# Gated linear attention issued by two generators, with level 2 of its scan issued beside level 4, a new order and overlap for the windowed attention, and separate tiles for one stage's norm factors

## The chip, the cores and the metric

One core of a Trainium2 chip runs the whole kernel. The metric is device time in microseconds (us) of one execution; lower is better. The kernel before takes 2370.8 us (median of three runs, 2370.01 to 2372.45).

## The reference

Two token sequences of width 1024, one of 2048 and one of 512 tokens, pass through two layers with the same weights, all in float32.

- Layer 0: one input projection feeds two attention branches. Branch A is gated linear attention: 4 heads of 128 channels, scanned forward and backward, each key weighted by a data-dependent decay: `scores[i,j] = sum_d q[i,d] k[j,d] exp(b[i,d] - b[j,d])`, where `b` is the running sum of the log decay; beyond a chunk the sum is carried by a state `S = exp(b_last) * S + k^T v`. Branch B is softmax attention over a window of 128 tokens to either side: 8 query heads share 2 key/value heads, with a relative-position bias and a sink logit. Each branch is multiplied by its own SiLU gate, and both go through one output projection.
- Layer 1: `y = W_out( silu(z) * B * conv3(C * h) )` with a depthwise convolution of width 3 along the tokens.
- After each layer: `x = LayerNorm(alpha * x + sublayer(x)) * g + b`, with the layer's own g and b.

## The kernel before, in words

**Work and tiles.** The 2560 tokens are five groups of 512 (group 4 is the short sequence) and 20 chunks of 128. Every dense projection is done in fp32r as three products: a matrix is cast to a high part (`wh`, or `hi` of the activations), the rest is a low part (`wl`, `lo`), and high*high, low*high and high*low are summed in PSUM. A step of 128x512 is one TensorE matmul; nearly all of the matmuls are of this form.

**The dense order.** `run` (L2103) has a fixed list of stages: for each group from 4 to 0 a token projection (`tok`), then a channel projection (`ch`, 21 units of 24 matmuls); between these the output projection of group 4 (`oe4`); then layer 1 of group 4 (`one`), and `oe0`, `oo4`, `oe1`, `oe2`, `pair0`, `oe3`, `oo0`, `pair1`, `oo1`, `oo2`, `oo3`. `oe` and `oo` are output projections of layers 0 and 1; `pair` does layer 1's input projection for two groups by a Strassen-like scheme of 7 products.

**What fills in.** Everything else runs as Python generators beside the dense order. `Flow` keeps a model clock for each engine (`Model.note` adds fixed costs for each instruction). After every few dense matmuls `Flow.pump` (L337) lets each generator issue its next piece if the model says that its inputs are there and VectorE and ScalarE are not over 4 to 5 us ahead. So the program order on each engine is settled when the program is built; at run time each engine takes its instructions strictly in that order, TensorE too, and a matmul whose input is late holds up all that follow it. `new` and `take` hand out tiles of small rings by the model's idle times: `md` (8 tiles of 128x512, called `mids`), `y` (4 of 128x1024, called `large`), `P` (4), `ps` and `acc` (4 PSUM banks each).

**Gated linear attention.** `gla_stream` (L1454) takes the chunks backwards, 19 to 16 and 15 to 0, one after the other. `inside` (L1186) does a chunk: it forms `Q` (q times decay, both directions), then goes through the scan levels s = 1, 2, 4, 8, 16, 32, 64. At each level it issues a burst of narrow matmuls (`blocks`: 16 fp32 products of 32 rows by 32 columns, two instructions each), grows `K` and `Q` by the decay totals on VectorE, and selects the level's block into `acmp`. Level 8 is already put off: `qm`, a copy of `Q`, is taken by ScalarE and its 32 instructions are issued in the burst of level 16 (L1238, L1308). After level 64 the same generator goes on with the chunk's tail: it completes `A`, transposes `K` (`turn`, L1327), multiplies with `v`, and updates the state `S`. Only then does the next chunk's `Q` start. When a sequence is done, `along` (L1402) runs forward over it and writes `mix_s`.

**Windowed attention.** `swa_front` (L1510) takes a block of 128 queries, one key/value head at a time: scores on TensorE, bias and maximum on VectorE, exponentials on ScalarE. `best` (L1518) chooses the next block: highest group first, until the mark `done_e1_0` (the last projection of group 0 is stored), then lowest block first. `swa_back` (L1579) transposes each of the up to three 128-wide parts of P, splits it into `ph` and `pl`, and issues the value products of part n after the transposes of part n+1.

**Norms.** `norms` (L1700) normalizes a stage's four rows of tiles with `ln_g` and `ln_b`, two tiles for the layer in hand. `ln_load` (L729) reloads them after `x1_0` (to layer 1), after `y_4` (to layer 0) and after `x1_3` (to layer 1).

Of the kernel before, what the change touches and what calls it, by code (L numbers as in the profile page):

```python
# [10 lines left out]
F32 = mybir.dt.float32  # L11
# [251 lines left out]
class Flow:  # L263
# [32 lines left out]
    def flush(self, everything=False, name=None):  # L296
        now, keep = [], []
        for one in self.late:
            (now if everything or name in one[2] or (name is None and one[0] <= self.t) else keep).append(one)
        self.late = self.model.late = keep  # L300
        for one in now:
            one[1]()
# [74 lines left out]
class Trunk:  # L377
    def __init__(self, tc, nc, I, y_out, ctx):
# [35 lines left out]
        self.blocks = []  # L414
# [3 lines left out]
        self.normed, self.turn = None, 0  # L418
# [150 lines left out]
    def dense_ch(self, xh, xl, w=None, last=True):  # L569
# [3 lines left out]
        p = self.pd()  # L573
# [13 lines left out]
        if last:  # L587
            self.drop(wl)
        return p
# [86 lines left out]
    def setup(self):  # L676
# [9 lines left out]
        self.dtot = c.tile([128, NC, 4], F32, name="dtot")  # L686
# [29 lines left out]
    def setup_late(self):  # L716
# [10 lines left out]
        yield from self.ln_load(0)  # L727

    def ln_load(self, layer):  # L729
        for t, n in zip(self.ln, ("ln_g", "ln_b")):  # L730
            yield from self.calm()
            self.nc.sync.dma_start(t[:], self.I[n][layer:layer + 1].broadcast_to([128, D]))
# [446 lines left out]

    def gla_load_k(self, c):  # L1180
        K = self.e((128, 2, 512), "KK")
# [4 lines left out]
    def inside(self, c, first, last, ld, K, ahead):  # L1186
# [3 lines left out]
        Q = self.e((128, 2, 512), "QQ")  # L1190
# [10 lines left out]

        acmp = self.sm((128, 4, 32), "acmp")
# [17 lines left out]
        def grow_k(s):  # L1220
# [12 lines left out]
        Sb = self.bst if not last else None  # L1233
        wait = []
        for li, s in enumerate((1, 2, 4, 8, 16, 32, 64)):
            n = 512 // s
            pls = []
            if s in (8,):  # L1238
# [3 lines left out]
            else:  # L1242
# [14 lines left out]
                for lt, t, qm in wait:  # L1257
# [3 lines left out]
                    self.drop(qm)  # L1261
# [24 lines left out]
                kms.pop(s, None)  # L1286
# [14 lines left out]
            if s not in (8,):  # L1301
                grow_q()
# [5 lines left out]
            if s in (8,):  # L1308
                grow_q()
# [13 lines left out]
        nc.vector.tensor_copy(self.dtot[:, c], mk(end, 4, [[1, 4]]))  # L1323
        ahead(0)
        self.flow.defer(lambda: nc.sync.dma_start(self.qf_s[c], Q[:, 1]), Q)

        def turn(i):  # L1327
# [3 lines left out]
            t = self.e((128, 4, 128), "km", bufs=2)  # L1331
# [3 lines left out]
        def grow(t):  # L1335
            pv = self.pw((128, 4, 128))
            for h in range(4):
                nc.tensor.matmul(pv[:, h], t[:, h], v[:, h * 128:h * 128 + 128], start=True, stop=True)
            return pv

        kf = kb = None
        if not last:
            yield from self.bank()
# [5 lines left out]
                                  acmp[:].unsqueeze(2).broadcast_to(wide))  # L1349
        if not first:  # L1350
            yield from self.bank()
            kb = turn(1)
        ahead(1)
# [10 lines left out]
        if not first:  # L1364
# [6 lines left out]
            else:  # L1371
                for h in range(4):
                    nc.vector.scalar_tensor_tensor(Sn[:, h], Sb[:, h], mk(end, h, [[1, 1]]), pv[:, h],
# [8 lines left out]
        yield [Q]  # L1382
# [19 lines left out]
    def along(self, c, first, last, ld, ahead):  # L1402
# [13 lines left out]
        if not last:  # L1416
# [4 lines left out]
            else:  # L1421
                for h in range(4):
                    nc.vector.scalar_tensor_tensor(Sn[:, h], Sf[:, h], self.dtot[:, c, h:h + 1], m[:, h],
# [29 lines left out]

    def gla_stream(self):  # L1454
        for g in (4, 3, 2, 1, 0):
# [3 lines left out]
            cs = list(range(4 * g + 3, 4 * g - 1, -1))  # L1459
            ld, K = self.gla_load(cs[0]), self.gla_load_k(cs[0])  # L1460
            nxt = {}
            for i, c in enumerate(cs):
                yield [*ld, K]

                def ahead(n):
                    if i < 3:
                        nxt[n] = (self.gla_load, self.gla_load_k)[n](cs[i + 1])
                yield from self.inside(c, *ends(c), ld, K, ahead)
                ld, K = nxt.get(0), nxt.get(1)
            if 4 * g > c0:  # L1470
                continue
            self.bst = None
            ld = K = None
            nxt.clear()
# [35 lines left out]
    def swa_front(self):  # L1510
# [7 lines left out]
        def best():  # L1518
# [4 lines left out]
            key = (lambda c: c) if "done_e1_0" in done else (lambda c: (-(c // 4), c))  # L1523
# [3 lines left out]
        while left:  # L1527
# [10 lines left out]
            for kv in range(2):  # L1538
# [3 lines left out]
                Pt = self.e((128, 4, 385), "P", bufs=4)  # L1542
# [36 lines left out]
    def swa_back(self):  # L1579
# [17 lines left out]
        for n in range(40):  # L1597
# [19 lines left out]
            old = None  # L1617
            for kb in range(nk):
# [586 lines left out]
```

## Time and profile before

| | |
|---|---|
| runs, median of 3 | 2370.8 us |
| the profiled execution's own time | 2370.12 us |
| its span, first to last instruction | 2368.1 us |
| TensorE matmul busy | 2343.9 us, 99% |
| TensorE weight loads busy | 1951.8 us, 82% |
| VectorE / ScalarE / GpSimd busy | 1582.8 / 1226.1 / 1418.4 us |

PE is TensorE, DVE VectorE, ACT ScalarE, POOL GpSimd, SPq the queue of SyncE, which issues the DMAs. Matmuls are pipelined, and the duration shown for one includes its time in the pipeline: what one costs is read from start to start, and "busy" does not mean that the engine advances at full rate.

### The profile page before, as it was taken

What the parts mean: (1) busy time and instruction counts of PE and PEld (TensorE: products, weight loads), DVE (VectorE), ACT (ScalarE), POOL (GpSimd) and SP (SyncE); (2) the same over time, 40 slices, a digit from 0 to 9 for tenths busy, and PEclk for the clock granted to TensorE, in tenths of its full rate; (3) what the DMA queues carried; (4) which work ended last, traced back from release to release, by engine and by line L of the source; (5) the groups of instructions that cost most, each with busy time, mean ns of one, the idle gap of its engine ahead of it and who ended that gap; (6) DMA issues with size and microseconds to landing.
All of it is one profiled execution on the core that took longest, in us unless ns stands there. A gap on an engine that the chain in (4) does not pass through costs nothing.

```text
span 2368.1 us, 43087 instructions
## 1 busy us (share of the span) xinstructions
PE 2343.9 (99%) x15830; PEld 1951.8 (82%) x15830; DVE 1582.8 (67%) x2699; ACT 1226.1 (52%) x2363; POOL 1418.4 (60%) x1610
## 2 busy tenths in 40 slices
PE   8999999999999999999999999999999999999998
PEld 8888889888988888888888888878888877888887
DVE  2267756767767677577776467876566587656567
ACT  4666776656576645665577532543334343333431
POOL 5454435443444444444444467898887689988674
PEclk9999999999999999999999999999999999999999
DMA  7977686676667657675478777232124633221573
GB/s 230 295 226 233 221 269 229 209 221 221 218 194 236 223 173 242 197 218 161 158 245 268 266 261 243 92 116 89 52 78 140 217 105 103 73 72 58 175 242 121
DMA packets 275057, 437.37 MB, mean 185 GB/s; under 512 B 21360, under 2 KB 160240, under 8 KB 274848
## 3 DMA queue, kind: packets, MB, share of 16 engines
q1 hardware_dynamic: 274848, 434.64, 56.5%
q8 instruction: 125, 2.05, 0.4%
q14 instruction: 84, 0.69, 0.1%
HBM read 319.72 MB, written 114.84 MB: 184 GB/s over the span
## 4 chain that ended last, share of the span: by engine, by line
PE 87%; DVE 5%; POOL 4%; DMA 2%; issue 1%; ACT 1%; SPq 0%; POOLq 0%; DVEq 0%; ACTq 0%
PE acc L242 71%; PE ps L242 17%; POOL wl L242 1%; POOL wh L242 1%; DVE st L242 1%; DVE bst L242 1%; DVE y L242 1%; POOL md L242 0%; SPq L242 0%; DVE QQ L242 0%; DVE P L242 0%; DVE KK L242 0%; DMA K<-kb_s 0%; DMA mix_s<-gb 0%; DMA op_s<-QQ 0%
## 5 line engine op out<-in xcount | busy, mean ns | idle before, releaser
L242 POOL TENSOR_TENSOR wl<-ws,wh 128x256 fp32r<-128x256 f32 (+1 forms) x912 | 750.7, 855 | 711.4 <-PE acc L242 478.0
L242 PE MATMUL acc<-st,wh 128*128 128x512 f32 x3160 | 828.5, 395 | 2.8 <-DVE pr L242 2.0
L242 PEld LDWEIGHTS acc<-st,wh 128*128 128x128 f32 x3160 | 580.9, 188 | 121.0 <-issue 3.1
L242 PE MATMUL acc<-st,wl 128*128 128x512 f32 x1744 | 471.9, 395 | 2.8 <-POOL wl L242 1.9
L242 PE MATMUL acc<-wh,st 128*128 128x512 f32 (+1 forms) x1680 | 389.4, 371 | 7.9 <-ACT st L242 6.4
L242 PEld LDWEIGHTS acc<-st,wl 128*128 128x128 f32 x1744 | 320.8, 188 | 68.0 <-POOL wl L242 4.1
L242 PEld LDWEIGHTS acc<-wh,st 128*128 128x128 f32 x1680 | 300.2, 189 | 55.1 <-ACT st L242 6.4
L242 ACT CAST wh<-ws 128x1024 fp32r<-128x1024 f32 (+2 forms) x252 | 249.0, 989 | 184.2 <-DMA ws<-in_w_oo 55.9
L242 PE MATMUL acc<-wl,st 128*128 128x512 f32 (+1 forms) x840 | 209.0, 368 | 0.6 <-POOL wl L242 0.5
L242 ACT ACTIVATE md<-md 128x512 f32<-128x512 f32 x264 | 164.7, 631 | 20.5 <-DVE md L242 14.9
L242 PEld LDWEIGHTS acc<-wl,st 128*128 128x128 f32 x840 | 150.7, 188 | 23.8 <-POOL wl L242 1.3
L242 DVE SCALAR_TENSOR_TENSOR md<-acc,md 128x512 f32<-128x512 f32 (+1 forms) x113 | 77.0, 683 | 81.5 <-ACT md L242 76.5
L242 DVE TENSOR_TENSOR st<-pr,st 128x512 fp32r<-128x512 f32 x115 | 98.5, 874 | 41.6 <-ACT st L242 41.2
L242 ACT ACTIVATE md<-acc 128x512 f32<-128x512 f32 (+1 forms) x133 | 76.2, 597 | 67.0 <-PE acc L242 66.5
L242 POOL TENSOR_TENSOR wh<-md,wh 128x256 fp32r<-128x256 f32 x118 | 96.7, 842 | 13.6 <-ACT wh L242 13.1
L242 ACT CAST pth<-ps 128x512 fp32r<-128x512 f32 x112 | 65.3, 583 | 73.1 <-PE ps L242 72.3
L242 DVE CUSTOM_DVE_ANT_0 P<-ps,P 128x384 f32<-128x384 f32 (+1 forms) x160 | 79.3, 525 | 29.6 <-PE ps L242 29.0
L242 ACT ACTIVATE P<-P,nm 128x385 f32<-128x385 f32 (+1 forms) x160 | 93.2, 587 | 3.9 <-DVE nm L242 3.9
L242 ACT ACTIVATE mv<-mv,eps 128x1 f32<-128x1 f32 x40 | 11.8, 295 | 151.8 <-DVE mv L242 147.7
L242 PE MATMUL acc<-P,wh 128*128 128x512 f32 x312 | 89.5, 400 | 0.4 <-POOL wh L242 0.4
L242 ACT COPY km<-KK 128x512 f32<-128x512 f32 x80 | 50.8, 635 | 72.2 <-DVE KK L242 50.9
L242 ACT CAST st<-pr 128x512 fp32r<-128x512 f32 x115 | 68.3, 617 | 30.3 <-DMA pr<-mix_s 12.9
(490 smaller groups left out, 4090.2 us busy)
## 6 DMA issues: line engine op xcount, KB each, us to landing
ws<-in_w_ch SPq DMA_DIRECT2D x105, 512.0 KB, 4.4
ws<-in_w_od SPq DMA_DIRECT2D x58, 512.0 KB, 4.2
ws<-in_w_oe SPq DMA_DIRECT2D x40, 512.0 KB, 3.8
ws<-in_w_oo SPq DMA_DIRECT2D x36, 512.0 KB, 3.5
K<-kb_s SPq DMA_DIRECT2D x32, 384.0 KB, 6.3
d_s<-md SPq DMA_DIRECT2D x40, 256.0 KB, 4.2
qb_s<-md SPq DMA_DIRECT2D x80, 128.0 KB, 3.9
tA<-d_s SPq DMA_DIRECT2D x20, 512.0 KB, 5.7
```

What stands on the lines that cost most here:

```text
L242: r = f(*a, **k)
```

## The change

- `inside` now ends after level 64 and puts what the tail needs on a list; a second generator, `gla_behind`, does the tails (`behind`). So the head of the next chunk may run beside the tail of this one. At most two chunks are open between head and the completed `A`.
- Level 2 is treated as level 8 was: `qm` is copied by ScalarE, and level 2's 32 instructions are issued in the burst of level 4.
- `Q` and `K` of a chunk may live in a `y` tile when their own tile is in use; copies of `K` and its transposes come from `md` tiles; loads of q, decay and `K` are issued from levels 4 and 32, the load of `v` by the tail.
- `swa_front` changes to lowest block first at `swa_in0` (the windowed attention's inputs of group 0 are stored), earlier than before. `swa_back` may have two transposed parts under way, and issues a part's value products after its own split.
- Layer 1's norm factors for the stage `y_4` get two `P` tiles of their own (`ln1`), filled after `x1_0`; the reload after `y_4` goes away.
- Some tiles are held explicitly, and `flush` no longer runs an entry twice.

```diff
@@ gla_home, gla_load_k
+    def gla_home(self, tag):
+        done = self.flow.done
+        rows = "swa_in1" in done and "res_x1_4_3" not in done
+        return [(self.e2, tag, 1)] if rows or self.model.spare(tag, 1) else self.large[:1]
-        K = self.e((128, 2, 512), "KK")
+        K = self.take(self.gla_home("KK"), (128, 2, 512))
@@ inside
-        Q = self.e((128, 2, 512), "QQ")
+        while self.free_at(self.gla_home("QQ")) > self.flow.t:
+            yield 0.3
+        Q = self.take(self.gla_home("QQ"), (128, 2, 512))
...
+        while self.open > 1:
+            yield 0.3
+        self.open += 1
...
-                    km = kms[2 * s] = self.e((128, 512), "km", bufs=2)
+                    km = kms[2 * s] = self.take([(self.e2, "km", 2)] + self.mids, (128, 512))
...
-            if s in (8,):
+            if s in (2, 8,):
+                while self.free_at(self.mids) > self.flow.t:
+                    yield 0.3
                 qm = self.m2(hold=True)
...
-            if s not in (8,):
+            if s not in (2, 8,):
                 grow_q()
...
-            if s in (8,):
+            if s in (2, 8,):
                 grow_q()
...
-            if s == 4:
-                v = self.e((128, 512), "v")
-                nc.sync.dma_start(v[:], self.v_s[c])
+            if s in (4, 32):
+                ahead(s)
             yield [Q] if s < 16 else [Q, K]
-        end = tots[128]
+        nc.vector.tensor_copy(self.dtot[:, c], mk(tots[128], 0, [[1, 8]]))
+        self.heads.append((c, first, last, K, Q, base, acmp))
+        self.flow.mark("head_%d" % c)
+    def behind(self, c, first, last, K, Q, base, acmp, v, ahead):
...
-            t = self.e((128, 4, 128), "km", bufs=2)
+            t = self.m2((128, 4, 128), hold=True)
@@ gla_behind
+    def gla_behind(self):
+        nxt = []
+        for c in [*range(19, 15, -1), *range(15, -1, -1)]:
+            yield "head_%d" % c
+            v = nxt.pop() if nxt else self.load_v(c)
+            def ahead():
+                if c not in (0, 16) and "gla_in%d" % ((c - 1) // 4) in self.flow.done:
+                    nxt.append(self.load_v(c - 1))
+            yield from self.behind(*self.heads.pop(0), v, ahead)
@@ swa_front
-            key = (lambda c: c) if "done_e1_0" in done else (lambda c: (-(c // 4), c))
+            key = (lambda c: c) if "swa_in0" in done else (lambda c: (-(c // 4), c))
@@ swa_back
+            def room():
+                return begun < nk and self.model.spare("ps", 4) > 1 and self.free_at([(self.pside, "ps", 4)]) <= self.flow.t
             for kb in range(nk):
+                if not turned:
+                    yield from self.bank()
+                    turn()
+                    begun += 1
+                if room():
+                    turn()
+                    begun += 1
+                pt, ph = turned.pop(0)
+                yield [ph]
...
+                yield [pl, V]
+                value(kb, ph, pl)
@@ norm, norms
-        g, b = self.ln
+        g, b = self.ln1 if one and one[:4] == "y_4_" else self.ln
...
-        if key in ("x1_0", "y_4", "x1_3"):
-            yield from self.ln_load(0 if key == "y_4" else 1)
+        if key == "x1_0":
+            yield "swa_all"
+            for n in range(2):
+                while self.free_at([(self.e2, "P", 4)]) > self.flow.t:
+                    yield 0.4
+                self.ln1.append(self.take([(self.e2, "P", 4)], (128, D)))
+            yield from self.ln_load(1, self.ln1)
+        if key == "y_4":
+            self.drop(*self.ln1)
+        if key == "x1_3":
+            yield from self.ln_load(1, self.ln)
@@ run
         flow.add(self.gla_stream(), rank=1)
+        flow.add(self.gla_behind(), rank=1)
```

## Rows read from the trace of the kernel before

**Rows 1.** The page, busy time, share of the span and instructions of each engine.

```profile
PE 2343.9 (99%) x15830; PEld 1951.8 (82%) x15830; DVE 1582.8 (67%) x2699; ACT 1226.1 (52%) x2363; POOL 1418.4 (60%) x1610
```

**Rows 2.** The page, the chain that ended last, by engine.

```profile
PE 87%; DVE 5%; POOL 4%; DMA 2%; issue 1%; ACT 1%; SPq 0%; POOLq 0%; DVEq 0%; ACTq 0%
```

**Rows 3.** Busy time by stretch: stretch, its length, each engine, PE clock, DMA.

```profile
118.00:355.00 237.00, 237.00 (x2134) 200.75 (x2133) 160.83 (x355) 163.51 (x354) 108.87 (x139) 1.00 0.75 238
355.00:1180.00 825.00, 823.14 (x7857) 691.13 (x7856) 596.59 (x1245) 499.45 (x969) 367.85 (x458) 1.00 0.66 208
```

**Rows 4.** The same view, a stretch of dense work alone.

```profile
1652.00:1711.00 59.00, 59.00 (x260) 48.33 (x259) 33.51 (x42) 23.24 (x33) 48.02 (x51) 1.00 0.18 62
```

**Rows 5.** PE in order of time (start, us, instructions): levels 2 and 4 of a chunk.

```profile
125.78 1.29 PE L242 MATMUL acc<-st,wh 128*128 128x512 f32 x5
127.01 0.46 PE L242 MATMUL ps<-QQ,km 128*32 128x32 f32 x32
127.40 2.11 PE L242 MATMUL acc<-st,wh 128*128 128x512 f32 x8
129.34 1.98 PE L242 MATMUL acc<-st,wl 128*128 128x512 f32 x8
131.25 0.46 PE L242 MATMUL ps<-QQ,km 128*32 128x32 f32 x32
```

**Rows 6.** The same view: levels 8 and 16 of that chunk, in one burst.

```profile
146.50 0.46 PE L242 MATMUL ps<-md,km 128*32 128x32 f32 x32
146.78 0.49 PE L242 MATMUL ps<-QQ,km 128*32 128x32 f32 x32
147.19 0.74 PE L242 MATMUL ps<-K,Q 128*128 128x256 f32 x4
```

**Rows 7.** Groups of PE instructions: count, busy and mean, idle before.

```profile
L242 PE MATMUL ps<-QQ,km 128*32 128x32 f32 x1920 | 28.1, 199 | 1.1 <-ACT pth L242 0.7 <-DVE acmp L242 0.2 <-DVE QQ L242 0.2
```

**Rows 8.** PE in order of time: 128-column products of a tail, then value products.

```profile
301.55 1.06 PE L242 MATMUL ps<-v,km 128*128 128x128 f32 x8
302.36 0.48 PE L242 MATMUL ps<-pth,V 128*128 128x512 f32 x1
302.68 0.40 PE L242 MATMUL ps<-ptl,V 128*128 128x512 f32 x1
```

**Rows 9.** What PE waited for from 118 to 1357 us: total, times, longest.

```profile
PE ps L242 <- ACT pth L242: 0.7, 1, 0.7
...
PE ps L242 <- DVE QQ L242: 0.2, 1, 0.2
```

**Rows 10.** Groups of ACT instructions: the copy of Q that puts level 8 off.

```profile
L242 ACT COPY md<-QQ 128x512 f32<-128x512 f32 x20 | 12.4, 619 | 0.0
```

**Rows 11.** Groups of DVE instructions, one operand in PSUM, then none.

```profile
L242 DVE TENSOR_TENSOR ptl<-ps,pth 128x512 fp32r<-128x512 f32 x112 | 76.3, 681 | 10.8 <-ACT pth L242 10.5
L242 DVE TENSOR_TENSOR QQ<-QQ,tC 128x512 f32<-128x512 f32 x60 | 51.5, 859 | 39.7 <-PE ps L242 39.4
```

**Rows 12.** Busy time by stretch: the most crowded 12 us of VectorE.

```profile
1092.00:1104.00 12.00, 11.69 (x172) 9.00 (x172) 11.69 (x25) 4.73 (x8) 5.82 (x6) 1.00 0.25 71
```

**Rows 13.** SP's queue in order of time, the second reload for x1_1's norms.

```profile
1448.95 0.43 SPq L242 DMA_DIRECT2D ln_b<-in_ln_b  x1
```

**Rows 14.** DVE in order of time, the first use of a reloaded factor.

```profile
1457.87 1.28 DVE L242 SCALAR_TENSOR_TENSOR Q<-Q,mv,ln_g 128x1024 f32<-128x1024 f32 x1
```

**Rows 15.** PE in order of time, the start of pair 0.

```profile
1546.48 1.98 PE L242 MATMUL acc<-st,wl 128*128 128x512 f32 x8
1549.60 0.73 PE L242 MATMUL acc<-st,wl 128*128 128x512 f32 x2 [1.14 <-POOL wl L242]
1551.27 1.08 PE L242 MATMUL acc<-st,wl 128*128 128x512 f32 x2 [0.94 <-DVE acc L242]
1552.15 4.20 PE L242 MATMUL acc<-P,wh 128*128 128x512 f32 x12
...
1556.18 0.39 PE L242 MATMUL acc<-st,wh 128*128 128x512 f32 x1
```

More of the change, by code (lines that the diff above doesn't have):

```diff
@@ L296, in flush @@
     def flush(self, everything=False, name=None):
[L297 to L300, printed above, removed]
+        now = [one for one in self.late if everything or name in one[2] or (name is None and one[0] <= self.t)]
         for one in now:
-            one[1]()
+            if any(one is x for x in self.late):
+                self.late[:] = [x for x in self.late if x is not one]
+                one[1]()
     def force(self, *tiles):
@@ L726, in setup_late, with ln_load @@
         self.ln = [c.tile([128, D], F32, name=n) for n in ("ln_g", "ln_b")]
-        yield from self.ln_load(0)
-    def ln_load(self, layer):
-        for t, n in zip(self.ln, ("ln_g", "ln_b")):
+        yield from self.ln_load(0, self.ln)
+    def ln_load(self, layer, tiles):
+        for t, n in zip(tiles, ("ln_g", "ln_b")):
             yield from self.calm()
@@ L1338, in grow, with place @@
                 nc.tensor.matmul(pv[:, h], t[:, h], v[:, h * 128:h * 128 + 128], start=True, stop=True)
+            self.drop(t)
             return pv
+        def place():
+            yield from self.bank()
+            while self.free_at(self.mids) > self.flow.t:
+                yield 0.3
         kf = kb = None
         if not last:
-            yield from self.bank()
+            yield from place()
             kf = turn(0)
@@ L1349, in inside @@
                                   acmp[:].unsqueeze(2).broadcast_to(wide))
+        self.open -= 1
         if not first:
-            yield from self.bank()
+            yield from place()
             kb = turn(1)
-        ahead(1)
+        self.drop(K)
         yield [A, v] + ([Sb] if Sb is not None else [])
@@ L1381, in inside @@
             self.flow.defer(lambda: nc.sync.dma_start(self.m_s[c], A[:].rearrange("p h t -> p (h t)")), A)
-        yield [Q]
+        self.drop(Q)
+        ahead()
+        self.flow.mark("tail_%d" % c)
     def along_load(self, c, first, last):
@@ L1616, in value, with turn @@
                 nc.tensor.matmul(po[:], vv, pl[:], start=False, stop=(kb == nk - 1))
[L1617 to L1619 removed]
+            turned, begun = [], 0
+            def turn():
                 pt = self.pw((128, 4, 128), hold=True)
                 for gq in range(4):
[L1622 to L1633 removed]
@@ new lines, in swa_back @@
+            for kb in range(nk):
+                if not turned:
+                    yield from self.bank()
+                    turn()
[5 more added lines that the diff above has]
+                yield [ph]
+                pl = self.new(self.e2, (128, 512), F32R, "ptl", 2, True)
+                nc.vector.tensor_tensor(pl[:], pt[:].rearrange("p h t -> p (h t)"), ph[:].bitcast(F32), op=ALU.subtract)
+                self.drop(pt)
+                pt = None
+                if not turned and kb < nk - 1:
+                    yield []
+                    if room():
+                        turn()
+                        begun += 1
+                if kb == nk - 1:
+                    self.drop(Pt)
+                    Pt = None
+                    self.blocks.pop(0)
+                yield [pl, V]
+                value(kb, ph, pl)
+                self.drop(ph, pl)
+                ph = pl = None
```

81 lines of the change are left out of this document (42 added, 39 removed).

## The prediction

> **What bounds the kernel now.** I read the page's busy times first. TensorE's matmuls are busy for 2343.9 of 2368.1 us [rows 1], and the chain that ended last is TensorE for 87% [rows 2]. A better schedule can therefore win little by filling idle time, since only 24 us are idle. But busy is not the same as advancing at full rate, so I next read starts instead of durations. In a stretch of dense work alone 260 matmuls of 512 columns start in 59.00 us [rows 4], which is 0.227 us each. The table by stretch shows the two stretches of linear attention, 118 to 355 and 355 to 1180 us, with TensorE busy for 237.00 of 237 and 823.14 of 825 us, while VectorE is at 68% and 72% and ScalarE at 69% and 61% [rows 3]. So in these 1062 us TensorE's instructions are the bound, and what counts is how many there are and what each costs in its place; work on the other engines is free until it makes TensorE wait. It waits little: from 118 to 1357 us the trace has four waits, 0.7 us the longest and 0.2 the shortest, 1.6 in all [rows 9].
>
> The orders in time show what is slow without being a wait. Around a burst of 32 narrow matmuls [rows 5] five dense matmuls start at 125.78 and the burst at 127.01: 1.23 us for work of 1.135, so 0.095 for entering. The burst runs to 127.40, 0.39. The eight dense matmuls behind it take 1.94 instead of 1.815, 0.125 more, and the next burst comes after 1.91 for eight, again 0.095 for entering. A lone burst costs 0.095 + 0.39 + 0.125 = 0.61 us. Levels 8 and 16, which share a burst of 64, run from 146.50 to 147.19 [rows 6]: 0.69, and with the same entry and the same delay behind it (which these rows don't show for it) 0.91.
>
> **The change part by part.** The sum is made against the profiled execution, 2370.12 us: its span of 2368.1 and 2.0 around it. It is 0.7 below the median of the runs, 2370.8, and I add that at the end.
>
> *Level 2 beside level 4.* Level 2 has a burst of its own now; it will sit in level 4's. The instructions stay: the form has 1920 of them, three groups of 32 for each of 20 chunks (levels 2, 4 and 16) [rows 7]. Two lone bursts, 2 x 0.61 = 1.22, become one of 0.91: 0.31 us for each chunk, 20 x 0.31 = 6.2 us. All of it lies in stretches where TensorE is the bound, so all of it moves the end. It could be less if a joint burst delays the dense work behind it by more: the most that rows allow is that only one entry is saved, 20 x 0.095 = 1.9. I take 6.2, since levels 8 and 16 are the same construction.
>
> The rule that speaks against so much: the Trainium skill, TensorEngine Tiling (Array Packing), Key Properties, says that changing the tiling mode drains the TensorE, and TensorE: Matmul & The Clock Gate, Step-by-step, puts a drain at about 128 cycles. As an estimate from those pages two changes of mode fewer in each chunk are 2 x 0.053 x 20 = 2.1 us (at the 2.4 GHz level), and the sum by that would be 2369.6 with the crowding below. The rows show 0.095 + 0.125 around a lone burst, about twice two such drains, and 0.09 more within (two runs of 0.39 against one of 0.69), so I go by the rows.
>
> The edit adds 20 copies on ScalarE, 0.619 us each by the copy that level 8 already needs, 12.4 us [rows 10]. ScalarE's 39% of free time in the long stretch hides them; without that cover they would be at most 12.4.
>
> *Two generators.* No arithmetic is added. Heads follow each other sooner, tails run beside them, and linear attention gets done earlier. That alone earns nothing: the dense order is unchanged, and TensorE is full whether a burst comes now or later. What it can change is waits. VectorE's work comes closer together. In the most crowded 12 us, with VectorE busy for 11.69, TensorE was busy for 11.69 too, 0.31 lost [rows 12]; over the long stretch it lost 825 - 823.14 = 1.86, 0.03 in 12 us [rows 3]. The new waits stand on TensorE ahead of dense matmuls, everything behind them waits too. From below, the 1.6 us of waits [rows 9] could go. From above, each chunk could pay the longest, 20 x 0.7 = 14. I take three more such crowded stretches, +0.9, near the lower end, because a generator still issues only when the model clock finds its inputs ready.
>
> *Tiles and loads.* `Q` and `K` may take `y` tiles and the turned `K` takes `md` tiles; the loads of q, decay and `K` come earlier on SP's queue, the load of `v` later, in the same number. A load that waits for its tile holds up the weight loads queued behind it on SP, and then GpSimd's low parts and TensorE. The nearest row for a dense stage that lacks a weight's low part is 1.14 us, at the pair's start [rows 15]; once in each of the four token projections from group 3 to 0 that would be 4.6, so 0 to 4.6. I take 0: `Q`'s and `K`'s places are asked for before they are taken.
>
> *Windowed attention.* The number of transposes and value products stays. A tail's eight products of 128 columns and the value product behind them take 302.68 - 301.55 = 1.13 us [rows 8]; less 0.227 that is 0.11 for each, with no visible price for changing between these forms. So their order is worth 0 within TensorE; the ends are the same waits as above. Lowest block first from an earlier mark brings group 0's results sooner, but TensorE has no wait over 0.7 between 118 and 1357, and `oe0` begins before that; nothing there to win.
>
> *Own norm factors.* Two DMAs go, 512 KB each by the tile's size. The second was issued at 1448.95 [rows 13] and a reloaded factor first used at 1457.87, in a VectorE sequence without a gap [rows 14]. So the reload is hidden by the norms before it and `oe1`'s last evictions, and its going is worth 0; without that cover it would be at most the 8.92 us between the two rows. *Held accumulators and flush* add no instruction: 0, and TensorE waits for no bank in the four rows; one such wait would be the 0.94 for DVE's `acc` [rows 15].
>
> Sum: 2370.1 - 6.2 + 0.9 = 2364.8; with 0.7 to the median **2365.5 us**.
>
> **The rivals.**
>
> *A. The gain is eaten or smaller.* Either only entries are saved, 2370.8 - 1.9 + 0.9 = 2369.8 (the place of the skill's drain rule named above), or each chunk pays a new wait of 0.2, the shortest seen [rows 9], 2370.8 - 6.2 + 4.0 = 2368.6. For it: every chunk has new neighbours in the queues, and VectorE's operations on two SBUF tiles take 859 ns where one with an operand in PSUM takes 681 [rows 11], while the model's fixed price is the same for both. Against it: even at 97% VectorE the loss was 0.31 in 12 us.
>
> *B. VectorE becomes the bound where head and tail overlap; slower.* The place is TensorE's narrow bursts of levels 4 to 64, which need VectorE's newest `Q`, `K` and `acmp`. If the model places them too early, each chunk pays about the longest wait, 0.7: 20 x 0.7 = 14, 2370.8 - 6.2 + 14 = 2378.6. It decides from 0.31 a chunk on against the gain, and from (6.2 + 4.7)/20 = 0.55 on for a measurable loss. For it: the 859 against 681 ns, and waits that name `acmp` and `QQ`. Against it: VectorE at 72% leaves 228 us over the long stretch, and its total work does not grow.
>
> *C. The pair's start loses its stall.* From 1546.48 to 1556.18 there are 24 matmuls, worth 5.45 us, in 9.70 [rows 15]: 4.2 lost, to GpSimd's `wl`, VectorE's `acc`, and then to matmuls at 0.33 us each. If the changed order before it removes that: 2361.3. For it: the work in front of the pair loses a reload and changes tiles. Against it: neither waited-for item belongs to the reload or to attention.
>
> *D. The change doesn't do what it says:* if tiles are never free in time, heads and tails stay in sequence; then the +0.9 goes and the rest stands, 2364.6, within the forecast.
>
> **How the numbers follow.** Forecast (with D) 0.54, its own range 2362 to 2368.5; A 0.18; B 0.15; C 0.13. A measurement of this kernel can tell about 0.2%, 4.7 us, from no change, so faster means below 2366.1. Two thirds of the forecast lie there, 0.37, and with C 0.50; the rest of it, 0.17, and A are 0.35; slower is B, 0.15. For the range I take C's end with another 2 us of the waits that could go, 2359, and above it A and the lighter half of B, 2373.
>
> **What would show it.** Level 2 right: narrow matmuls of the form from an `md` copy double from 640 to 1280, those from `QQ` with `km` fall by 640, and 20 of the 32-bursts are gone, with about 6 us less between the starts of the dense stages on either side. Crowding: the waits of TensorE between 118 and 1357, now 1.6, and VectorE's share there; over 11 us more of waits means B. The reload: `x1_1`'s norms no earlier against the end of `oe1`. C: the 24 matmuls at the pair's start. I am wrong if the narrow bursts merge and the stretch up to 1357 doesn't get shorter, or if the end moves by more than 6 us for anything behind it.

## The result, and the profile after

The changed kernel takes 2374.88 us (median of 20 runs, 2371.47 to 2384.03), the kernel before 2369.94 beside it: ratio 1.0025, 95% interval 1.0019 to 1.0032. I had forecast 2365.5, so the change went the other way: 5 us slower in place of 5 us faster. Its profiled execution is one of the longest, 2380.03 us with a span of 2377.9 and a mean granted clock of 0.996, where the four executions at 0.999 took 2371.47 to 2373.13.

The page's busy row for the kernel after, against [rows 1]:

```profile
PE 2343.1 (99%) x15830; PEld 1958.0 (82%) x15830; DVE 1579.3 (66%) x2699; ACT 1235.1 (52%) x2384; POOL 1426.6 (60%) x1610
```

TensorE has the same 15830 matmuls and the same busy time in a longer span. The same stretches as in [rows 3], kernel after, show where it idles: 2.61 us of the first, 8.48 of the second, where before it was 0 and 1.86, with VectorE and ScalarE about as busy as before.

```profile
118.00:355.00 237.00, 234.39 (x2120) 199.66 (x2119) 158.09 (x348) 163.17 (x351) 107.96 (x139) 0.99 0.74 235
355.00:1180.00 825.00, 816.52 (x7831) 690.78 (x7830) 587.84 (x1236) 506.22 (x981) 369.68 (x453) 0.99 0.66 209
```

The join itself did what it should. TensorE in order of time in the same chunk as [rows 5], kernel after; levels 2 (`md`) and 4 (`QQ`) now share a burst:

```profile
132.25 2.43 PE L242 MATMUL acc<-st,wh 128*128 128x512 f32 x10
134.60 0.46 PE L242 MATMUL ps<-md,km 128*32 128x32 f32 x32
134.88 0.49 PE L242 MATMUL ps<-QQ,km 128*32 128x32 f32 x32
135.30 1.65 PE L242 MATMUL acc<-st,wh 128*128 128x512 f32 x6
136.79 1.98 PE L242 MATMUL acc<-st,wl 128*128 128x512 f32 x8
```

Ten dense matmuls take 2.35 us to the burst (2.27 at 0.227 each), the burst 0.70, the six behind it 1.49 (1.362): 0.08 + 0.70 + 0.13 = 0.91, the joint price that I had put together from [rows 5, 6]. The groups of PE instructions, kernel after, show that it happened in all chunks: 1280 narrow matmuls read an `md` copy of Q, 640 before.

```profile
L242 PE MATMUL ps<-md 128*32 128x32 f32 x640 | 9.4, 201 | 0.0
L242 PE MATMUL ps<-md,km 128*32 128x32 f32 x640 | 9.2, 199 | 0.0
```

The bursts merged, and TensorE's idle time in the two stretches grew by 9.2 us, more than the join gives: the sign by which I had said that I would be wrong.

What took it back are waits of PE. The four longest groups of eight, 118 to 1360 us, kernel after (total, times, longest); the eight are 11.8 us, before there were four of 1.6 in all [rows 9]:

```profile
PE acc L242 <- DVE md L242: 4.0, 1, 4.0
PE ps L242 <- DMA K<-kb_s: 2.7, 2, 1.8
PE ps L242 <- DVE y L242: 2.1, 1, 2.1
PE ps L242 <- DVE ptl L242: 1.1, 2, 0.9
```

To add up gains and losses I took from each trace the interval from every matmul's start to the next, less the usual one of its shape (0.227 us for 128x512 [rows 4], 0.153 for 128x336, 0.007 for a narrow one). *Narrow* is what this leaves around and in the narrow bursts (32 and 64 columns wide); *late* is the sum of all intervals more than 0.18 us too long, most of them waits, some of them matmuls at a lower clock. A *place* is a group of late starts close together.

| profiled execution | narrow | late, 118 to 1360 | late, elsewhere | small rest | last matmul starts |
|---|---|---|---|---|---|
| before | 56.3 | 3.0 | 13.7 | 22.5 | 2359.9 |
| after | 51.2 | 16.8 | 14.5 | 23.0 | 2369.7 |
| difference | -5.1 | +13.8 | +0.8 | +0.5 | +9.8 |

(The first matmul starts 0.3 earlier.) This is the profiled execution, 10 us over the one before. The medians are only 4.9 apart, so with the same 5.1 gained an estimate of the loss at the median is about 10. Three places make 12.0 of the 16.8. In each, one matmul at the head of TensorE's queue waits for its input, and everything behind it waits too.

*172 us, 2.3.* PE in order of time, kernel after (start, us, instructions, [idle before <- releaser]):

```profile
172.32 0.46 PE L242 MATMUL ps<-md,km 128*32 128x32 f32 x32
174.84 0.46 PE L242 MATMUL ps<-y,km 128*32 128x32 f32 x32 [2.07 <-DVE y L242]
175.23 0.58 PE L242 MATMUL acc<-wl,st 128*128 128x336 f32 x2
```

VectorE there, kernel after:

```profile
171.07 0.16 DVE L242 SCALAR_TENSOR_TENSOR nm<-mx,nsink 128x4 f32<-128x4 f32 x1
171.16 1.39 DVE L242 SCALAR_TENSOR_TENSOR md<-acc,norm_g,md 128x512 f32<-128x512 f32 x2
172.48 0.55 DVE L242 TENSOR_TENSOR tC<-tB 128x256 f32<-128x256 f32 x1
173.50 0.69 DVE L242 TENSOR_TENSOR y<-y,tC 128x512 f32<-128x512 f32 x1 [0.47 <-DVE tC L242]
174.10 0.68 DVE L242 TENSOR_TENSOR y<-y,tB 128x512 f32<-128x512 f32 x1
```

A joint burst: its level 2 half is issued, its level 4 half needs `Q` (here in a `y` tile) grown by `tB`. That stands on VectorE behind two operations of the dense stage's SiLU and behind the growth of `K` by `tC`, which the edit puts ahead of `Q`'s at level 2. The two growths themselves take 0.69 and 0.68 us. Busy time by stretch behind the wait, kernel after (stretch, length, PE, weight loads, DVE, ACT, POOL, PE clock, DMA):

```profile
174.80:176.00 1.20, 1.16 (x36) 1.07 (x37) 1.17 (x4) 0.86 (x2) 0.00 (x0) 1.00 0.98 297
176.00:178.00 2.00, 2.00 (x10) 1.95 (x9) 2.00 (x6) 1.14 (x4) 0.00 (x0) 0.57 0.23 80
178.00:180.00 2.00, 2.00 (x10) 2.00 (x9) 1.86 (x5) 1.30 (x3) 1.92 (x3) 0.58 0.40 118
```

The wait costs more than itself: after 1.2 us at full clock the granted clock is 0.57 and 0.58 for 4 us.

*378 us, 5.2.* PE in order of time, kernel after:

```profile
377.93 0.86 PE L242 MATMUL acc<-wh,st 128*128 128x336 f32 x4
382.76 1.49 PE L242 MATMUL acc<-wh,st 128*128 128x336 f32 x4 [3.96 <-DVE md L242]
```

VectorE there, kernel after:

```profile
378.19 0.85 DVE L242 TENSOR_TENSOR KK<-KK,tC 128x512 f32<-128x512 f32 x1
378.97 1.03 DVE L242 TENSOR_TENSOR QQ<-QQ,tB 128x512 f32<-128x512 f32 x1
379.92 0.68 DVE L242 SCALAR_TENSOR_TENSOR md<-acc,md 128x512 f32<-128x512 f32 x1
380.52 0.14 DVE L242 SCALAR_TENSOR_TENSOR nm<-mx,nsink 128x4 f32<-128x4 f32 x1
380.59 0.68 DVE L242 SCALAR_TENSOR_TENSOR md<-acc,md 128x512 f32<-128x512 f32 x1
381.96 1.41 DVE L242 SCALAR_TENSOR_TENSOR md<-acc,norm_g,md 128x512 f32<-128x512 f32 x2 [0.69 <-ACT md L242]
```

The token projection needs an accumulator that the SiLU chain of the channel projection still holds; the chain waits on VectorE behind the first head of a group, which grows `KK` and `QQ`. Here too the clock falls. The same view:

```profile
378.00:382.70 4.70, 0.80 (x6) 0.51 (x4) 3.90 (x8) 3.53 (x7) 1.44 (x2) 0.83 0.18 59
382.70:387.00 4.30, 4.24 (x75) 3.82 (x75) 2.52 (x5) 3.18 (x10) 0.00 (x0) 0.50 0.75 163
387.00:391.00 4.00, 4.00 (x23) 3.80 (x24) 3.82 (x8) 2.42 (x4) 2.39 (x4) 0.89 0.93 297
```

The granted clock falls during the wait and is 0.50, the 1.2 GHz level, for the 4.3 us after it, where the four 128x336 products at 382.76 need 1.29 us in place of 0.61.

*1035 us, 4.5.* PE in order of time, kernel after:

```profile
1034.80 1.07 PE L242 MATMUL acc<-st,wl 128*128 128x512 f32 x4
1037.71 0.36 PE L242 MATMUL ps<-K,Q 128*128 128x256 f32 x1 [1.84 <-DMA K<-kb_s]
1038.90 0.86 PE L242 MATMUL ps<-K,Q 128*128 128x256 f32 x5 [0.83 <-DMA K<-kb_s]
```

SP's queue before it, kernel after:

```profile
1032.59 1.22 SPq L242 DMA_DIRECT2D K<-kb_s  x2
1033.92 0.54 SPq L242 DMA_DIRECT2D ws<-in_w_ch  x1
1034.50 0.43 SPq L242 DMA_DIRECT2D gb_s<-md  x1
1034.97 1.60 SPq L242 DMA_DIRECT2D y<-k_s  x2
```

The two loads of the windowed attention's keys were issued at 1032.59 and 1033.20, and the matmuls that need them start at 1037.7 and 1038.9: 5.1 and 5.7 us, beside a head's `K` (`y<-k_s`) and a weight. That is no slow load: the 40 loads `K<-kb_s` of this trace land 3.9/6.6/7.2 us (min/median/max) after their issue, and in the kernel before 5.1/6.4/8.6. The model clock takes at least 3.6 for a load (a constant in `Model.note`), less than any of them. The waits are 2.67 of the 4.5; behind them the clock falls again:

```profile
1040.00:1045.00 5.00, 5.00 (x30) 3.94 (x30) 3.94 (x13) 2.99 (x6) 1.71 (x1) 0.67 0.91 335
```

The three waits are 8.7 us. The lower clock behind them costs about 5.9, an estimate from the five stretches shown behind the waits (what is missing to 1.00, times the length). Only part of that is over 0.18 us in one interval and so in *late*. The kernel before has a clock of 1.00 in all of [rows 3].

### The profile page after: what moved, and what is told of

Its sections match the earlier page's. It is cut to its first block, busy times and chain, and to the rows that moved or that the text cites. A ratio compares the mean times of both kernels' runs of the same rounds, so it can differ in the third digit from the quotient of the medians.

```text
span 2377.9 us, 43080 instructions
## 1 busy us (share of the span) xinstructions
PE 2343.1 (99%) x15830; PEld 1958.0 (82%) x15830; DVE 1579.3 (66%) x2699; ACT 1235.1 (52%) x2384; POOL 1426.6 (60%) x1610
## 3 DMA queue, kind: packets, MB, share of 16 engines
q1 hardware_dynamic: 274704, 433.59, 56.5%
## 4 chain that ended last, share of the span: by engine, by line
PE 87%; DVE 5%; POOL 3%; DMA 2%; issue 1%; SPq 1%; ACT 1%; POOLq 0%; DVEq 0%; ACTq 0%
PE acc L242 71%; PE ps L242 17%; POOL wl L242 1%; DVE st L242 1%; POOL wh L242 1%; DVE y L242 1%; DVE bst L242 1%; DVE QQ L242 1%; SPq L242 1%; DVE KK L242 1%; POOL md L242 0%; DVE md L242 0%; DVE P L242 0%; DMA ws<-in_w_ch 0%; DMA pr<-in_xT 0%
## 5 line engine op out<-in xcount | busy, mean ns | idle before, releaser
L242 PE MATMUL acc<-st,wl 128*128 128x512 f32 x1744 | 465.3, 395 | 2.7 <-POOL wl L242 2.7
L242 PE MATMUL acc<-wh,st 128*128 128x512 f32 (+1 forms) x1648 | 383.3, 371 | 12.8 <-ACT st L242 6.9
L242 ACT ACTIVATE P<-P,nm 128x385 f32<-128x385 f32 (+1 forms) x160 | 93.2, 588 | 10.6 <-DVE nm L242 10.6
L242 ACT ACTIVATE mv<-mv,eps 128x1 f32<-128x1 f32 x40 | 11.8, 294 | 148.7 <-DVE mv L242 148.7
L242 ACT CAST wh<-md 128x512 fp32r<-128x512 f32 x59 | 36.5, 620 | 100.6 <-PE acc L242 40.2
L242 DVE TENSOR_TENSOR ptl<-ps,pth 128x512 fp32r<-128x512 f32 x112 | 75.3, 681 | 18.4 <-ACT pth L242 18.2
```

What stands on the lines that cost most here:

```text
L242: r = f(*a, **k)
```

## The experiments

Theory 1 as it stood for e1 to e5: the join is worth its 5 to 6 us, and the overlap of heads and tails crowds VectorE and ScalarE, so that fixed places of the program order are late and take back more. Rivals: the join makes its own late starts; the windowed attention's change does; a load lands late by chance. From e7 on the theory is narrower: the places arise where the model prices too little. The before runs beside the groups of experiments gave 2369.86, 2369.54, 2368.84 and 2369.13 us. All runs at a glance (interval of the ratio to before in brackets; late starts as above; places of more than 1.5 us between 118 and 1360):

| run | us | ratio | narrow | late 118 to 1360 | late 1360 to 1600 | places |
|---|---|---|---|---|---|---|
| before | 2369.94 | 1 | 56.3 | 3.0 | 6.1 | none |
| after | 2374.88 | 1.0025 [1.0019, 1.0032] | 51.2 | 16.8 | 6.4 | 172, 378, 1035 |
| e1 | 2375.89 | 1.0025 [1.0016, 1.0033] | 51.0 | 16.2 | 6.2 | 171, 375, 1032 |
| e2 | 2437.06 | 1.0283 [1.0265, 1.0300] | 50.7 | 39.2 | 34.0 | many |
| e3 | 2370.36 | 1.0001 [0.9993, 1.0010] | 50.6 | 9.2 | 3.8 | 167, 900 |
| e4 | 2378.55 | 1.0037 [1.0023, 1.0051] | 50.8 | 16.6 | 4.5 | 173, 372, 596, 815, 1340 |
| e5 | 2373.04 | 1.0019 [1.0009, 1.0029] | 56.6 | 8.4 | 4.4 | 815 |
| e6 | 2368.77 | 0.9998 [0.9989, 1.0007] | 50.7 | 7.4 | 5.5 | 171, 1120 |
| e7 | 2366.30 | 0.9990 [0.9981, 0.9999] | 50.7 | 7.2 | 3.0 | 620 |
| e8 | 2384.17 | 1.0066 [1.0054, 1.0077] | 50.7 | 7.8 | 18.9 | 319 |
| e9 | 2369.99 | 1.0002 [0.9993, 1.0011] | 50.4 | 5.7 | 11.3 | 1013 |
| e10 | 2363.07 | 0.9981 [0.9972, 0.9991] | 56.6 | 1.4 | 4.7 | none |
| e11 | 2417.58 | 1.0211 [1.0197, 1.0225] | 56.5 | 29.1 | 20.3 | many |
| e12 | 2358.22 | 0.9954 [0.9942, 0.9967] | 50.9 | 2.8 | 3.1 | 1023 |
| e13 | 2370.95 | 1.0002 [0.9993, 1.0011] | 56.5 | 6.6 | 4.8 | 374, 635 |
| e14 | 2364.21 | 0.9977 [0.9968, 0.9986] | 50.5 | 6.8 | 3.0 | 806, 1017 |
| e15 | 2387.26 | 1.0072 [1.0057, 1.0088] | 56.6 | 4.2 | 19.8 | 892 |
| e16 | 2363.74 | 0.9973 [0.9965, 0.9981] | 50.8 | 2.5 | 5.6 | none |

**e1, the changed kernel again.**

> The changed kernel once more, for a second profile of it. Its first profile lost 12.8 us between 355 and 1180 us to starts of TensorE that came more than 0.18 us late (3.0 before the change), most at 172 (VectorE's y), 378 (VectorE's md) and 1035 us (the load of K). Theory 1, the order of the program is too dense for VectorE and ScalarE: the same places are late again, within 1 us each, and the ratio is 1.0025. Theory 2, chance arrivals of DMAs: other places are late, with a like sum. The run's time should lie between 2371 and 2384.

The three places come back within 4 us of their times, and each within 0.4 us of its size. They belong to the program order; the load at 1035 us isn't chance.

**e2, the kernel before with the join alone.** Only the `s in (2, 8)` edits, `km` in an `md` tile, in one generator.

> The kernel before with level 2 issued in level 4's burst, and nothing else. If the gain of the joint burst is as sized (0.31 us a chunk) and the joint burst brings no waits of its own: 2370 - 6 = 2364, ratio 0.9975, 100 narrow bursts instead of 120. If the later level 2 itself makes TensorE wait (it joins a burst that needs two copies by ScalarE and a Q two steps further): late starts between 118 and 1180 rise from 3 to about 10 us and the ratio is 0.999 to 1.002.

Both missed: it is 67 us slower than before. The bursts get their gain (50.7) and late starts up to 1180 us stay at 3.1, but a joined chunk takes longer from head to head: the last head ends at 1288 us in place of 1170, the forward pass at 1460 in place of 1357, and the output projections, which stand in the fixed dense order, wait for it. PE's waits, 1180 to 1600 us, of e2:

```profile
PE ps L242 <- ACT km L242: 23.7, 6, 5.9
PE ps L242 <- DVE md L242: 7.5, 1, 7.5
PE acc L242 <- ACT st L242: 7.3, 2, 6.0
```

So when linear attention ends isn't free, as "earns nothing" had it. Which part of the change makes the join affordable isn't shown by this: e3 has heads and tails in series too, and does not pay it.

**e3, heads only after the tail before them.**

```diff
                 yield [*ld, K]
+                if c < c1 - 1:
+                    yield "tail_%d" % (c + 1)
```

(and four free `P` tiles asked for at the pair's start, which this order needs.)

> The changed kernel, but a chunk's head starts only when the tail of the chunk before it is done (the pair's preparation also waits until its four P tiles are free). Theory 1, the overlap of heads and tails crowds VectorE and ScalarE: the late starts fall from 16 us back to about 4, the gain of the joint bursts stays, 2363 to 2366, ratio 0.997 to 0.9985. Rival, the windowed attention's new order and turns are the cause: the ratio stays at 1.002 to 1.003, and the late starts before the loads of K remain.

4.5 us faster than the change, but theory 1's range is missed: late starts fall to 9.2, not 4, with two places over 2.5 us elsewhere. By the last product of `v` and `A` in a tail and the first burst of the next head, 12 of 19 tails end inside the next head in the change, none here and none before. So the overlap may cost up to 4.5 us in this order, and the join in series is affordable beside the rest of the change: the last head ends at 1208 us, the forward pass at 1418, and the projections behind it lose 3.8 us.

**e4, the windowed attention as before** (order by `done_e1_0`, parts turned one after the other).

> The changed kernel with the windowed attention as before (blocks in the old order until group 0's last projection is stored, value products of a part behind the transposes of the next). Rival, the windowed attention is the cause: ratio 0.997 to 0.9985. Theory 1, the overlap of heads and tails is the cause: ratio 1.001 to 1.004, and late starts of 10 us or more between 118 and 1180 us.

No faster, and with 10.8 us of late starts up to 1180 us, as theory 1 had it. The place at 1035 us goes, others come (815, 1340 us). So that change isn't the cause of the loss as a whole.

**e5, no join.**

```diff
-            if s in (2, 8,):
+            if s in (8,):
-            if s not in (2, 8,):
+            if s not in (8,):
```

> The changed kernel with level 2 in a burst of its own again; the two generators and all else stay. Theory 1 (overlap of heads and tails makes the late starts): the gain of the joint bursts goes, narrow bursts cost 5 to 6 us more, the late starts between 118 and 1180 us stay at 12 to 16 us, 2380 to 2382. Rival (the longer chain of level 2, by two copies of ScalarE and a late Q, makes the late starts): they fall by 6 us or more, level 4's wait at 172 us among them, and the time stays at 2374 to 2376 or falls.

Narrow bursts lose the gain again, +5.4, but half of the late starts go, 16.8 to 8.4, the places at 172 and 1035 us among them. The net is 1.8, and theory 1's 2380 to 2382 is missed. In this order the join brings late starts of its own, as its rival had it.

**e6, a group's first head 14 us later.**

```diff
             yield "gla_in%d" % g
+            if g < 4:
+                yield 14.0
```

> The changed kernel, but the linear attention waits 14 us after the inputs of each of the groups 3 to 0 are stored. If a group's first head, whose first VectorE operations stand in front of the SiLU operations that free the accumulators for the token projection, causes the 4.1 us late start at 378 us: that one and the 1 us behind it go, 2370 to 2371. Rival (it moves elsewhere, since VectorE has as much to do): the sum of late starts stays within 2 us, 2374 to 2377.

The place at 378 us goes, as the theory on that place said, and the time falls by 6 us, to 1 below the forecast's range. But the place at 1035 us shrinks too, to 1.4, so the 6 us aren't that place's alone.

**e7, a better price for VectorE.**

```diff
-            return n / 960 + (0.155 if len(outs) < 2 else 0.23), 0.06
+            two = len(ins) > 1 and not any(x.tensor.name.startswith(("acc_", "ps_")) for x in outs + ins)
+            return n / 960 + (0.155 if len(outs) < 2 else 0.23) + (0.15 if two and n > 256 else 0.0), 0.06
```

> The changed kernel with one number of the model raised: a VectorE operation with two operands in SBUF and over 256 elements a partition costs 0.15 us more in the model, nearer to the 0.78 to 0.86 us that the trace shows for 512 elements. If too low a price for VectorE places TensorE's narrow bursts too early: the late starts of 118 to 1180 us fall from 15.8 to 8 or less, 2367 to 2369. Rival (the late starts come from waits that the price doesn't reach: SiLU chains through two engines, the arrival of DMAs): they stay at 12 or more, 2372 to 2377.

All three places go, the one that waits for a load among them, one of 5.1 comes at 620 us, and the time falls by 8.6 us against the change, though the price touches no arithmetic, only the order of it. The model has 512/960 + 0.155 = 0.69 us for a 128x512 operation on two SBUF tiles; the trace of the changed kernel (min/median/max of two forms, in ns) says:

```profile
L242 DVE TENSOR_TENSOR QQ<-QQ,tB x33: 679/1022/1233, 133.2 to 1110.0; 128x512 f32<-128x512 f32 x33
L242 DVE TENSOR_TENSOR QQ<-QQ,tC x33: 676/692/1228, 136.1 to 1115.3; 128x512 f32<-128x512 f32 x33
```

So the old price is right for most of the second form and too low for most of the first. No single price fits both.

**e8, shorter lead of the two generators** (2.5 us ahead allowed, not 4).

> The changed kernel, but the two linear attention generators issue only while the model finds VectorE and ScalarE at most 2.5 us ahead of TensorE, instead of 4.0. If long queues on these engines in front of dense work cause the late starts: those of 118 to 1180 us fall to 8 us or less, 2367 to 2370. Rival: the linear attention gets slower, and its end makes the output projections wait, as where level 2 was joined alone: over 2376. Second rival: no change within 2 us.

The rival is right: late starts in attention fall to 7.8, but the last head ends at 1231 us, and 18.9 us of late starts stand between 1360 and 1600.

**e9, e7's price and e6's later head.**

> The changed kernel with two edits at once: the model's higher price for VectorE operations on two SBUF tiles (e7, 2366.3) and the group's first head put 14 us later (e6, 2368.8). Theory (late starts are fixed places in the program order, made where the model prices too little): the place at 378 us that the later head removed is already gone with the price, so the two don't add; 2364 to 2368. Rival (each removes waits of its own): the gains against the changed kernel, 9 and 6 to 7, add, 2360. Second rival (any edit reshuffles the places by chance): anywhere from 2364 to 2374, with new late starts over 2 us at other times.

They don't add, and 2369.99 is above the theory's range. It is the second rival that came, with new places at other times: 2.9 at 1013 us, and 6.7 at 1388 where the forward pass ends late, at 1400. Late starts in attention are the fewest of the joined orders so far.

**e10, e7's price without the join; e11, e7's price in the kernel before; e12, e7's price and a higher price for loads:**

```diff
-            end = max(at + 3.6, self.bus + 1.8)
+            end = max(at + 5.0, self.bus + 1.8)
```

> The changed kernel with the higher VectorE price, and level 2 in its own burst again. Theory (the joint burst is worth its 5 to 6 us of TensorE's narrow bursts as soon as the late starts are priced away): 4 to 6 us above e7's 2366.3, so 2370 to 2372, narrow bursts 56 us against 51, late starts from 118 to 1360 about as many as e7's 7. Rival (the join itself makes matmuls late whatever the price, as e5 seemed to say): within 2 us of e7, 2364.5 to 2368, with fewer late starts than e7.

> The kernel before, with nothing but the higher VectorE price in the model (a control). Theory (the kernel before, in series, has next to no late start in attention that a better price could remove, 3 us from 118 to 1360): within 2 us of 2369.9, so that e7's lead is due to the change with its late starts gone. Rival (the price helps any order): 2364 to 2367, and the change is still worth nothing. A third way: the price holds the serial stream back, linear attention ends later, and the projections behind it wait: over 2375.

> The changed kernel with the higher VectorE price, and a DMA's least time in the model at 5.0 us in place of 3.6 (the load of K that made TensorE late at 1035 us landed later than the model thought). Theory: waits of TensorE for DMA vanish, which e7 has nearly none of from 118 to 1360, so it stays within 2 us of e7, 2364.5 to 2368. Rival (longer assumed loads hold the two generators back as the shorter lead did): linear attention's last head ends after 1180 us and the time is 2370 or more.

e10 met its rival, below even e7: 5.9 us more in the bursts, 5.8 fewer late in attention. e11 took its third way: a dearer VectorE makes the serial stream slow (last head 1247 us). e12 is the best of all, 10.6 us below before, outside both ranges. Its busy time by stretch, against the rows of after above:

```profile
118.00:355.00 237.00, 236.78 (x2132) 200.90 (x2132) 160.52 (x349) 162.87 (x342) 113.22 (x143) 1.00 0.74 239
355.00:1180.00 825.00, 823.19 (x7889) 697.07 (x7889) 602.62 (x1242) 513.36 (x1013) 372.32 (x459) 1.00 0.67 212
```

TensorE loses 2.03 us of both stretches (11.09 in after), while VectorE is busier over the two than in either kernel: its load on the whole isn't the cause.

**e13 to e16: both prices without the join; the load price alone; that in the kernel before; both prices with 4.3 in place of 5.0.**

> e12 (both prices, 2358.2) with level 2 in its own burst again. Theory (the joint burst is worth its 5 to 6 us when few starts are late either way): 2363 to 2365, narrow bursts 56 to 57 us against 50.9, late starts from 118 to 1360 within 3 us of e12's 2.8. Rival (the join always costs in late starts what it gains): 2356.5 to 2360.5.

> The changed kernel with only the DMA's least time in the model raised, 3.6 to 5.0 us. Theory (most late starts come from VectorE's price, the load at 1035 us from this one): the places at 172 and 378 us stay (2.2 and 4.1), the one at 1035 us goes, 2369 to 2372. Rival (longer loads alone loosen the heads enough to remove all): 2358 to 2362.

> The kernel before with only the DMA's least time in the model raised, 3.6 to 5.0 us (a control). Theory: nothing waits for a DMA there between 118 and 1360 us, so 2368 to 2372, unless the serial heads get slower, then over 2372. Rival (the load price helps any order, and e12's lead isn't the change's): 2358 to 2364.

> e12 with the DMA's least time at 4.3 us in place of 5.0. Theory (the prices remove the late starts because they are nearer to the real ones, so a nearby value does nearly as well): 2358 to 2364, late starts from 118 to 1360 at most 6 us. Rival (e12 is one lucky order among many whose places fall by chance): 2364 to 2372.

e13 is 12.7 us above e12 and outside both ranges; 5.6 are the bursts, 3.8 late starts in attention, most of them in two places. The larger one, TensorE in order of time, e13:

```profile
373.58 0.77 PE L243 MATMUL ps<-wh,st 128*128 128x336 f32 x4
377.01 0.85 PE L243 MATMUL ps<-wh,st 128*128 128x336 f32 x4 [2.65 <-DVE acmp L243]
```

e14 missed both ways: the load price alone removes the places at 172 and 378 us, leaves 1.6 of that at 1035 (here 1017), and takes 10.7 us off the change's time. Those two wait for VectorE and not for a load, as e7's price removed a wait for a load: a price need not be that of the late item to move a place. e15: the kernel before gets 18 us slower by it (last head 1199 us), so not every order gains from it. e16 is 5.5 above e12 and just within the theory's range.

## Why the prediction was wrong

**What bounds the kernel** held, with one gap. TensorE's starts are the bound, but not only through the work on them: linear attention must also end before the output projections in the dense order. I had said that its getting done earlier earns nothing; its being late goes with 67 us in e2 (the forward pass ends at 1460) and 15 in e8, both against the kernel before, while e3's end at 1418 costs nothing there.

**Level 2 beside level 4** was right, and 1 us too large: -6.2 forecast, -5.1 in the profiled execution and -5.3 in e1; in the pairs with and without the join (e5 and after, e10 and e7, e13 and e12) 5.4, 5.9 and 5.6. This also settles rival A's first half: only entries saved would be 1.9. Narrow bursts went from 56.3 to 51.2. By the Trainium skill's drain (TensorEngine Tiling (Array Packing), Key Properties), which I had put at an estimate of 2.1 us, they would be at 54.2, so the measurement decides against that price. The added copies are there (ScalarE +9.0 us and 21 instructions), and no wait of TensorE between 118 and 1360 us names them.

**The step that failed is "+0.9", the crowding of the two generators.** I took three more stretches like [rows 12] because "a generator still issues only when the model clock finds its inputs ready". It was 13.8 in the profiled execution and about 10 at the median. That reason is what failed: at 172 and 1035 us a piece was issued whose input came 2.1 and 2.7 us too late for a queue that can't overtake. At 378 us a head's own inputs were there, but its work on VectorE stands in front of the dense stage's SiLU, which a look at its inputs doesn't see. The upper bound that I gave, 14, has the size, but not the shape: not 0.7 for each of 20 chunks, which was rival B, but three places of 2.3, 5.2 and 4.5. That B's end, 2378.6, is near the result is luck: VectorE was no busier than before, and in e12 it is busier still while TensorE hardly waits. I also had no term for the clock, about 5.9 us behind the three waits. Why the model is early at a place is argued and not shown. A price too low fits 1035 us (3.6, where no load took under 3.9) and 378 (0.85 and 1.03 us in front of the SiLU chain, priced at 0.69), but not 172, where the growths took what the model says. [rows 11], which I had used for a rival and not for the term, I misread: 859 ns is a mean, and those 60 operations take 640/692/1795 (min/median/max), so most cost the model's price and some far more.

**Tiles and loads**, taken at 0 of 0 to 4.6: no wait for linear attention's held-up weights, which I had named, is among the long ones. The 4.5 at 1035 us are the windowed attention's keys, and since e4, e5 and e7 each remove that place, it isn't shown to be any one edit's.

**Windowed attention, own norm factors, held accumulators:** e4 shows no loss from the first. Between 1360 and 1600 us late starts are 6.4 against 6.1 before, so the reload was hidden, as forecast. *C* didn't come. TensorE at the pair's start, kernel after, against [rows 15]:

```profile
1558.00 1.98 PE L242 MATMUL acc<-st,wl 128*128 128x512 f32 x8
1561.88 1.92 PE L242 MATMUL acc<-st,wl 128*128 128x512 f32 x4 [1.91 <-POOL wl L242]
1563.59 3.81 PE L242 MATMUL acc<-P,wh 128*128 128x512 f32 x12
1567.24 0.39 PE L242 MATMUL acc<-st,wh 128*128 128x512 f32 x1
```

24 matmuls in 9.24 us, 9.70 before. The matmuls "at 0.33 us each" of [rows 15] are the lower clock: from 1551 to 1555 us it was 0.57. *D* didn't come either: 12 of 19 tails end inside the next head.

**What is shown and what isn't.** Shown: the join's gain in the bursts; that the loss lies in late starts that repeat, and in the lower clock behind them; that changing nothing but the model's prices takes the places at 172 and 378 us and most of that at 1035 away and makes the same arithmetic 8.6 (e7) to 16.7 us (e12) faster. Not shown: that the prices work by being truer. Every new order has its own places: e10 and e13 differ by the load price alone and by 7.9 us, the wrong way round, and the join's whole effect is -12.7 (e13 to e12), +1.8 (e5 to after) and +3.2 (e10 to e7), -2.6 on average. So the join's worth in the end time isn't shown either, only its gain in the bursts. The five orders with the join and a raised price (e7, e9, e12, e14, e16) average 2364.5, which is 1.0 below my forecast; but a single order of this program lies some 6 us to either side, and these five were made to lose the late starts, so that this agreement is partly luck.

## What to carry to other kernels

Where a program order is fixed at build time by a cost model, a change that saves instructions' time also draws a new order, and here that alone moved the time of the changed kernel by 8.6 to 16.7 us (e7, e14, e12), more than the change itself. Price such a change in two terms, the local gain and the re-drawn waits, and test it by the same change under two or three slightly different prices. Before you call work "off the critical path", look for the stage in the fixed order that will one day wait for its end.

## What the runs showed of the hardware

After a wait in an otherwise full stream, TensorE's granted clock can fall to 0.50, its 1.2 GHz level, for some microseconds. In the profiled execution of the changed kernel it did so behind all three places, among them one of 2.07 us: 0.57 and 0.58 from 176 to 180 us, 0.50 from 382.7 to 387, 0.67 from 1040 to 1045. At 382.76 that is 1.29 us for work of 0.61. It differs between executions: in e1 the clock stays at 1.00 from 174.8 to 180 us behind the same first wait, and behind the other two it is 0.51 from 381 to 384.4 and 0.50 from 1036.5 to 1039.5.

One and the same VectorE operation on two SBUF tiles, 128x512 in float32, takes from 0.68 to 1.23 us within one execution, with a median of 1.02 for one form and 0.69 for another. The 40 loads of the windowed attention's keys land 3.9 to 7.2 us after their issue in one execution, half of them after 6.6 us or more.
